# Layer 0's MLP with both token streams in shared tiles and joint groups of 512 columns

## The chip, the cores and the metric

The kernel runs on one core of one Trainium2 chip. The metric is device time in microseconds of one execution; several executions are timed and their median is given. One further execution is profiled, and all rows in this document come from such profiles. TensorE multiplies matrices and writes PSUM, VectorE (DVE) and ScalarE (ACT) do elementwise work, GpSimd (POOL) does little here, and SyncE (SP) issues the DMAs.

## The reference

A backbone of two layers works on two streams of 256 tokens each with 1024 channels: context tokens and latent tokens. Each layer has a mixing part (three head groups: differential attention, latent attention, an RWKV-7 scan) and then a channel part, a gated MLP with a centred convolution of width 3 over the tokens:

```python
def conv_ffn(h, P):
    u = dwconv3(h @ P['ffn_w_up'], P['ffn_conv_w'], P['ffn_conv_b'])
    g, v = jnp.split(u, 2, axis=-1)
    return (jax.nn.silu(g) * v) @ P['ffn_w_down']
```

The up weight has 1024 rows and 2 x 2816 columns, the down weight 2816 rows and 1024 columns. Both streams use the same weights of a layer, each with its own normalisation and modulation before it. Latents read the context in the mixing part, the context never reads the latents, and after layer 1 only the latents are returned, so layer 0 runs its MLP on both streams and layer 1 only on the latents.

## The kernel before, in words

**Layout and arithmetic.** Channels lie on the 128 partitions, tokens on the free axis. Every fp32 operand is split in a high part `h` and a low part `lo` of the type fp32r, and a product is three matmuls, high by high, high by low, low by high (`mm3`, lines 277 to 279). A weight tile of 128x1024 is loaded by SyncE, cast to its high part on ScalarE (line 269) and subtracted to its low part on VectorE (line 270), in `wgroup`.

**The MLP's groups.** `ffn` (line 1176) goes through 22 groups `i` of 128 gate columns and the 128 value columns that belong to them. For each group it makes g (8 k-tiles x 3 matmuls), then v (the same), into one PSUM bank: g in columns 0 to 255, v in 256 to 511. `tap3` (line 449) reads each half out of PSUM: one activation with scale and bias on ScalarE (line 454) and two multiply-adds with shifted tokens on VectorE (lines 457 and 458). Then come silu on ScalarE (1244), the product on VectorE (1245), a cast to the high part (223) and the low part (1247), which give the group's "act". Two groups later the act is multiplied with its 128 rows of the down weight (`push`, `second`): 4 quarters (2 token halves x 2 column halves, one accumulating bank each) x 3 matmuls of 512 columns. The last four rows of the down weight are held to the end and then done quarter by quarter; each quarter ends with `finish`.

**The two streams.** The first call, `ffn(0, hc, ...)`, runs all 22 groups for the context. Beside it a generator (`Side`, line 1266) does what is left of the latents' mixing part, five steps for each group, and ends with the latents' own normalisation (`normed` at line 1541, `norm_mod` at line 405), which makes `hl`. From group `JOIN` = 11 on, that generator is run to its end, and each group is done for both streams with one loading and splitting of the up weights: the context's g and v in a bank of tag `g`, the latents' in a bank of tag `r`. The order within such a group is g of the context, g of the latents, v of the context, v of the latents, each of 24 matmuls with 256 moving columns. Acts of the latents are kept in tiles of tag `al`. The second call, `ffn(0, hl, ..., early=ahead)`, does the latents' groups 0 to 10 and takes the other acts from there; beside it the context's part of layer 1 runs.

**Memory.** `hc` and `hl` of layer 0 are four tiles each, `[128, 4, 256]`, two k-tiles of high and of low part in one (`stream_h`, line 399). Tags name groups of buffers, `BUFS` (line 103) their counts; PSUM has two banks of tag `g`, two of `r`, four of `acc` (the quarters) besides those of the attention (`PB`, line 108).

**What sets the order.** The program's text names no order between engines. A planner takes all instructions with modelled costs, starts on each engine what is ready and most urgent, and places tiles of all tags in one memory by lifetimes; a tile that needs a buffer waits for its release. So independent chains are interleaved on an engine. The resulting order on each engine is fixed in the program. Accesses to parts of one SBUF tile that don't overlap are not ordered against each other; in PSUM, accesses to one bank are. Some loads are tied to a matmul by hand: the loads of layer 1's first weights wait for the last up matmul of the fourth group from the end (`marks[-4]`, group 18).

Of the kernel before, what the change touches and what calls it, by code (L numbers as in the profile page):

```python
# [10 lines left out]
F32 = mybir.dt.float32  # L11
F32R = mybir.dt.float32r
I32 = mybir.dt.int32
AF = mybir.ActivationFunctionType
ALU = mybir.AluOpType
# [4 lines left out]
P = 128  # L20
DM = 1024
KT = DM // P
# [69 lines left out]
def tile_trunk(ctx: ExitStack, tc, A, out):  # L92
# [7 lines left out]
        uid[0] += 1  # L100
        return f"{s}_{uid[0]}"

    BUFS = dict(h=8, hc=4, hl=4, otc=4, otl=4, wrs=13, wrm=3, whm=3, wlm=4, wro=4, who=5, wlo=3, wra=4, wrf=3, whf=4, wlf=6, at=4, al=4, c4=12, d4=12, rk=4, xsc=2, xsd=2, xn=2, nf=5, xs=4, ar=3, gv=3, pa=8, oh=2, sh=3, ob=1, stc=3, std=1, xt=4, gt=2, qk=2, qz=4, va=2, bm=3, lx=1, wx=1, vb=1, bq=3, pc=4)

    def T(tag, shape, dt=F32, pool=None):
        return sb.tile(shape, dt, tag=tag, name=nm(tag), bufs=BUFS[tag])

# [291 lines left out]
    def stream_h(tag):  # L399

        ts = [T(tag, [P, 4, SQ], F32R) for _ in range(KT // 2)]
        hs = [(t[:, 0:2], t[:, 2:4], t.bitcast(F32)[:, 0:2]) for t in ts]
        return hs, [(ts[k // 2][:, k % 2], ts[k // 2][:, 2 + k % 2]) for k in range(KT)]

    def norm_mod(hs, xns, sc, tags):

# [769 lines left out]
    def ffn(l, hk, gate, fill, other=None, early={}, begin=(0, nofill)):  # L1176
# [35 lines left out]
            else:  # L1212
                second(k, wg, quads)

        def place(name, tag):

            n, _, _ = slots.get(name, (0, 0, 0))
            if n % 2 == 0:
                gv, at = T("gv", [P, 4, SQ]), T(tag, [P, 4, SQ], F32R)
            else:  # L1220
                _, gv, at = slots[name]
            slots[name] = n + 1, gv, at
            n %= 2
            return gv[:, n * 2], gv[:, n * 2 + 1], at[:, n], at[:, 2 + n], at.bitcast(F32)[:, n]

        for n, i in enumerate(todo):
            if n == begin[0]:
                begin[1]()
                turn[0] = "acc"
                acc.extend([PS("acc") for _ in range(2)] for _ in range(2))  # L1230
            streams = [(hk, PS("g"), place(0, "at"), acts)]
            h2 = other(i) if other else None
            if h2:
                streams.append((h2, PS("r"), place(1, "al"), ahead))
            for gi, m in enumerate((i, NFF + i)):
                wg = wgroup(A["ffn_w_up"][l][:, m * P : (m + 1) * P].rearrange("(k p) c -> p k c", p=P), KT, P)
                for x, ps, at, _ in streams:
                    for k in range(KT):
                        ins = mm3(ps[:, gi * SQ : (gi + 1) * SQ], (wg[0][:, k, :], wg[1][:, k, :]), x[k], k == 0, k == KT - 1)
                    tap3(ps[:, gi * SQ : (gi + 1) * SQ], at[gi], 1, PPc(l, "cw0", m), PPc(l, "cw1", m), PPc(l, "cw2", m),  # L1240
                         PPc(l, "cb", m))
            marks.append(ins)
            for _, _, (g, v, h, lo, hf), res in streams:
                S.activation(g, g, AF.Silu)
                V.tensor_tensor(g, g, v, ALU.mult)
                copy("ffh", h, g)
                V.tensor_tensor(lo, g, hf, ALU.subtract)
                res[i] = h, lo
            fill()
            for k in order[n]:  # L1250
                push(k)
# [57 lines left out]
                V.scalar_tensor_tensor(xs[j], pcs[j], r[:, i : i + 1], xs[j], ALU.mult, ALU.add)  # L1309
        return xs  # L1310

    def normed(l, s, pcs, ssq, base, gname, tag, tags, each=False):
        xns = normalise(close(s, pcs, ssq, each), "xn", each)
        sc = modulation(l, base, gname, s)
        hs, hk = stream_h(tag)
        norm_mod(hs, xns, sc, tags)
        return hk

# [191 lines left out]
    def after_context(late):  # L1510

        saved = list(phase)
        phase[:] = ["o", late, 0]
        for ti in (0, 1):
            load_x(ti, True, late)
        gt = gate_tile(0, 2, CTX, late)
        out0["wo"], pcs, ssq = run(w_out(0, oTs[CTX], W0, gt, WO))
        for _ in range(NB):
            queue.append((1, (2, 3, 0, 1, 4, 5)[out0.setdefault("ada", 0)]))
            out0["ada"] += 1  # L1520
            fill()
        out0["hc"] = normed(0, CTX, pcs, ssq, 3, "fpre", "hc", NT, EA)
        turn[0] = HB
        phase[:] = saved

# [4 lines left out]
    def latents0():  # L1530
        while not (heads.done and mixing.done):
            heads.step()
            mixing.step(MIX)
            yield
        late = chain[LAT]
        phase[:] = ["o", late, 0]
        for ti in (2, 3):
            load_x(ti, True, late)
        gt = gate_tile(0, 2, LAT, late)
        late, pcs, ssq = yield from w_out(0, oTs[LAT], "r", gt, (2, 0, 1, 3))  # L1540
        return normed(0, LAT, pcs, ssq, 3, "fpre", "hl", ("r",), EB)


    hc, wo = out0["hc"], out0["wo"]
# [3 lines left out]
    def fill_side(n):  # L1548
        def f():
# [5 lines left out]
    agate[:] = [wo, 0]  # L1555
    queue.extend((1, ch) for ch in (2, 3, 0, 1, 4, 5)[NB:])
    marks, pcs, ssq, ahead = ffn(0, hc, lambda ins: gate_tile(0, 5, CTX, ins), fill_side(SB),
                                lambda i: side.run() if i >= JOIN else None, begin=(ACC0, heads.run))
    hl = side.run()


# [126 lines left out]
```

## Time and profile before

| | |
|---|---|
| time before, median of 3 runs | 1360.2 us (1359.5 to 1369.34) |
| the profiled execution's own time | 1361.95 us |
| its span, first to last instruction | 1360.1 us |
| mean granted TensorE clock | 0.981 of full speed |
| TensorE busy | 1285.8 us (95%) |
| VectorE busy | 965.8 us (71%) |
| ScalarE busy | 696.1 us (51%) |
| first joint matmul of the latents | 553.34 us after the start |
| last one of them | 702.38 us |

Busy time of an engine is the time in which it has an instruction running; matmuls overlap, so their durations add up to more than it. "Idle before" in a row is the time for which the engine had nothing, and behind the arrow stands what ended it. The granted clock is that of TensorE, 1.00 for its full speed.

### The profile page before, as it was taken

To read this page: it belongs to the slowest core of one execution; us is meant where nothing else is said; L and a number is where in the kernel's file an instruction comes from. 1 tells how busy PE (TensorE), PEld (TensorE's weight loads), DVE (VectorE), ACT (ScalarE), POOL (GpSimd) and SP (SyncE) were. 2 spreads that over 40 slices of the span, in tenths; PEclk is the share of its full clock that TensorE was granted. 3 is DMA by queue.
4 is the path that set the end of the run, shared out by engine and by line. 5 is a ranking of instruction groups with operands and counts; after the bars stand their busy time and mean duration, and the time that the engine had idled before them with its cause. 6 is when DMAs were issued, how large, how long until landed. Compare 5 with 4: busy or idle time off the path is not lost.

```text
span 1360.1 us, 27958 instructions
## 1 busy us (share of the span) xinstructions
PE 1285.8 (95%) x11208; PEld 1079.1 (79%) x11208; DVE 965.8 (71%) x2438; ACT 696.1 (51%) x1368; POOL 21.1 (2%) x41
## 2 busy tenths in 40 slices
PE   5999999998989999999999999999998997999997
PEld 4787766665777888999999888889865775999996
DVE  3548667657679587866769579587869587777776
ACT  4335244765664554534446555655545654555553
POOL 0001000000000000000000000000100000000000
PEclk9999899997999999999999999999998998999999
DMA  9830265300886565432557446447220048456662
GB/s 323 273 108 16 62 178 183 116 1 2 299 283 189 168 218 170 130 118 78 163 184 224 140 152 206 138 122 214 63 63 1 2 138 265 140 170 202 186 183 81
DMA packets 216531, 202.50 MB, mean 149 GB/s; under 512 B 7825, under 2 KB 175313, under 8 KB 216401
## 3 DMA queue, kind: packets, MB, share of 16 engines
q1 hardware_dynamic: 216400, 200.71, 47.6%
q8 instruction: 88, 1.44, 0.4%
q14 instruction: 43, 0.34, 0.1%
HBM read 198.55 MB, written 2.13 MB: 148 GB/s over the span
## 4 chain that ended last, share of the span: by engine, by line
PE 79%; DVE 13%; ACT 4%; issue 2%; DMA 1%; SPq 0%; POOL 0%; ACTq 0%; DVEq 0%; POOLq 0%
PE g L277 10%; PE g L279 10%; PE g L278 10%; PE acc L277 7%; PE acc L279 7%; PE acc L278 7%; PE r L277 3%; PE r L279 3%; PE r L278 3%; PE acc L906 3%; PE g L1103 2%; PE acc L902 1%; PE r L770 1%; PE r L789 1%; PE acc L322 1%
## 5 line engine op out<-in xcount | busy, mean ns | idle before, releaser
L270 DVE TENSOR_TENSOR wlf<-wrf,whf 128x1024 fp32r<-128x1024 f32 x176 | 214.3, 1220 | 58.8 <-ACT whf L269 37.2
L269 ACT ACTIVATE whf<-wrf 128x1024 fp32r<-128x1024 f32 x176 | 184.6, 1051 | 31.2 <-DMA wrf<-in_ffn_w_up_dram 8.6
L277 PE MATMUL g<-hl,whf 128*128 128x256 f32 x528 | 149.7, 285 | 0.9 <-DVE gv L458 0.8
L278 PE MATMUL g<-hl,whf 128*128 128x256 f32 x528 | 148.9, 284 | 0.0
L279 PE MATMUL g<-hl,wlf 128*128 128x256 f32 x528 | 147.0, 284 | 0.1
L454 ACT ACTIVATE gv<-g,pers 128x256 f32<-128x256 f32 x110 | 61.9, 563 | 155.6 <-PE g L279 154.6
L277 PEld LDWEIGHTS g<-hl,whf 128*128 128x128 f32 x528 | 100.9, 191 | 4.8 <-issue 2.2
L278 PEld LDWEIGHTS g<-hl,whf 128*128 128x128 f32 x528 | 101.0, 191 | 1.9 <-issue 0.3
L277 PE MATMUL g<-hc,whf 128*128 128x256 f32 x352 | 100.6, 286 | 1.6 <-DVE gv L458 0.9
L278 PE MATMUL g<-hc,whf 128*128 128x256 f32 x352 | 100.4, 285 | 0.0
L279 PEld LDWEIGHTS g<-hl,wlf 128*128 128x128 f32 x528 | 99.7, 191 | 1.0 <-issue 0.3
L279 PE MATMUL g<-hc,wlf 128*128 128x256 f32 x352 | 100.0, 285 | 0.0
L457 DVE SCALAR_TENSOR_TENSOR gv<-g,pers,gv 128x255 f32<-128x255 f32 x110 | 52.7, 479 | 65.5 <-ACT gv L454 65.5
L270 DVE TENSOR_TENSOR wlm<-wrm,whm 128x1024 fp32r<-128x1024 f32 (+2 forms) x64 | 71.9, 1132 | 33.3 <-ACT whm L269 19.6
L277 PE MATMUL acc<-whf,at 128*128 128x512 f32 x220 | 87.9, 402 | 0.4 <-ACT ar L344 0.4
L278 PE MATMUL acc<-wlf,at 128*128 128x512 f32 x220 | 87.5, 398 | 0.6 <-DVE wlf L270 0.6
L279 PE MATMUL acc<-whf,at 128*128 128x512 f32 x220 | 86.8, 395 | 0.1
L269 ACT ACTIVATE whm<-wrm 128x1024 fp32r<-128x1024 f32 (+2 forms) x64 | 62.5, 987 | 38.8 <-PE acc L279 17.4
L277 PEld LDWEIGHTS g<-hc,whf 128*128 128x128 f32 x352 | 67.2, 191 | 4.5 <-issue 2.5
L278 PEld LDWEIGHTS g<-hc,whf 128*128 128x128 f32 x352 | 67.2, 191 | 1.5 <-issue 0.2
L279 PEld LDWEIGHTS g<-hc,wlf 128*128 128x128 f32 x352 | 67.1, 191 | 0.4
L895 ACT ACTIVATE pa<-g,pers 128x512 f32<-128x512 f32 (+1 forms) x72 | 44.2, 615 | 32.9 <-DVE pers L894 32.4
(534 smaller groups left out, 3434.4 us busy)
## 6 DMA issues: line engine op xcount, KB each, us to landing
wrf<-in_ffn_w_up_dram SPq DMA_DIRECT2D x110, 512.0 KB
wra<-in_ada_w_dram SPq DMA_DIRECT2D x80, 512.0 KB
wrf<-in_ffn_w_down_dram SPq DMA_DIRECT2D x66, 512.0 KB
wrm<-in_w_in_dram SPq DMA_DIRECT2D x52, 512.0 KB
wro<-in_w_out_dram SPq DMA_DIRECT2D x24, 512.0 KB
wrs<-in_ada_w_dram SPq DMA_DIRECT2D x32, 256.0 KB
gt<-gate SPq DMA_DIRECT2D x6, 512.0 KB
wrm<-in_w_in_dram SPq DMA_DIRECT2D x8, 352.0 KB
```

The lines of the kernel that those rows point to most:

```text
L269: S.activation(h[:, :n], raw[:, :n], AF.Copy)
L270: V.tensor_tensor(lo[:, :n], raw[:, :n], h.bitcast(F32)[:, :n], ALU.subtract)
L277: first = TE.matmul(ps, lh[0], rh[0], start=start, stop=False)
L278: TE.matmul(ps, lh[0], rh[1], start=False, stop=False)
L279: TE.matmul(ps, lh[1], rh[0], start=False, stop=stop)
L322: ins = TE.matmul(ps[q * 32 : q * 32 + 32, :], ca[:, k, :], ws[k // 2][:, c0 : c0 + P], start=k == 0, stop=k == KT - 1)
L454: S.activation(o[:, : n * SQ], ps[:, : n * SQ], AF.Identity, scale=wc, bias=bias)
L457: V.scalar_tensor_tensor(o3[:, :, 1:SQ], p3[:, :, 0 : SQ - 1], wp, o3[:, :, 1:SQ], ALU.mult, ALU.add)
L770: chain[s] = TE.matmul(px[eo * 64 : eo * 64 + 64, pd, :], sc[:, pd, eo, 0:64], SV[:, pd, eo, :], start=True, stop=True)
L895: S.activation(pr_[:, :nk], ps[:, :nk], AF.Exp, bias=m, accum_out=sm)
L906: TE.matmul(po[:, :width], pT[:, b * P : (b + 1) * P], vtiles[b], start=(b == 0), stop=(b == nb - 1))
L1103: ins = TE.matmul(ps[:, :nk], qT[:, i, qc : qc + P], kT_[:, :nk], start=True, stop=True)
```

## The change

Layer 0's normalised input of both streams goes into shared tiles: `both_h` makes four pairs of tiles of a new tag `hj`, `[128, stream, k-tile, 256]`, one of a pair for high, one for low parts. Each stream has its view for its own normalisation and its own groups, and a third view takes a k-tile of both streams as 2 x 256 columns, with a gap between the two runs. `hj` has 8 buffers; `hc` and `hl` are used from layer 1 on.

In groups 11 to 21 a matmul now streams that third view, 512 columns, so that a group has 2 x 24 matmuls. The bank of tag `g` holds g of both streams, the bank of tag `r` holds v of both. Taps, activation and product run once over 512 columns in a new tile `[128, 2, 512]` of tag `gv`; cast and low part are still made per stream, into the same `at` and `al` tiles. The groups of one stream alone are as before.

```diff
--- before.py
+++ after.py
@@ -100,7 +100,7 @@
         uid[0] += 1
         return f"{s}_{uid[0]}"
 
-    BUFS = dict(h=8, hc=4, hl=4, otc=4, ...)
+    BUFS = dict(h=8, hc=4, hl=4, hj=8, otc=4, ...)
 
     def T(tag, shape, dt=F32, pool=None):
         return sb.tile(shape, dt, tag=tag, name=nm(tag), bufs=BUFS[tag])
@@ -401,6 +401,14 @@
         ts = [T(tag, [P, 4, SQ], F32R) for _ in range(KT // 2)]
         hs = [(t[:, 0:2], t[:, 2:4], t.bitcast(F32)[:, 0:2]) for t in ts]
         return hs, [(ts[k // 2][:, k % 2], ts[k // 2][:, 2 + k % 2]) for k in range(KT)]
+
+    def both_h():
+
+
+        ts = [(T("hj", [P, 2, 2, SQ], F32R), T("hj", [P, 2, 2, SQ], F32R)) for _ in range(KT // 2)]
+        views = [([(h[:, s], lo[:, s], h.bitcast(F32)[:, s]) for h, lo in ts],
+                  [(ts[k // 2][0][:, s, k % 2], ts[k // 2][1][:, s, k % 2]) for k in range(KT)]) for s in (CTX, LAT)]
+        return views, [(ts[k // 2][0][:, :, k % 2], ts[k // 2][1][:, :, k % 2]) for k in range(KT)]
 
     def norm_mod(hs, xns, sc, tags):
 
@@ -1212,39 +1220,50 @@
             else:
                 second(k, wg, quads)
 
-        def place(name, tag):
+        def place(name, tag, wide=False):
 
             n, _, _ = slots.get(name, (0, 0, 0))
             if n % 2 == 0:
-                gv, at = T("gv", [P, 4, SQ]), T(tag, [P, 4, SQ], F32R)
+                gv, at = None if wide else T("gv", [P, 4, SQ]), T(tag, [P, 4, SQ], F32R)
             else:
                 _, gv, at = slots[name]
+                if gv is None and not wide:
+                    gv = T("gv", [P, 4, SQ])
             slots[name] = n + 1, gv, at
             n %= 2
-            return gv[:, n * 2], gv[:, n * 2 + 1], at[:, n], at[:, 2 + n], at.bitcast(F32)[:, n]
+            act = at[:, n], at[:, 2 + n], at.bitcast(F32)[:, n]
+            return act if wide else (gv[:, n * 2], gv[:, n * 2 + 1]) + act
 
         for n, i in enumerate(todo):
             if n == begin[0]:
                 begin[1]()
                 turn[0] = "acc"
                 acc.extend([PS("acc") for _ in range(2)] for _ in range(2))
-            streams = [(hk, PS("g"), place(0, "at"), acts)]
-            h2 = other(i) if other else None
-            if h2:
-                streams.append((h2, PS("r"), place(1, "al"), ahead))
-            for gi, m in enumerate((i, NFF + i)):
+            both = other(i) if other else None
+            if both:
+                gv = T("gv", [P, 2, 512])
+                g, v = gv[:, 0], gv[:, 1]
+                outs = [(place(0, "at", True), acts), (place(1, "al", True), ahead)]
+                parts = [(PS("g"), g), (PS("r"), v)]
+            else:
+                g, v, *act = place(0, "at")
+                outs = [(act, acts)]
+                ps = PS("g")
+                parts = [(ps[:, 0:SQ], g), (ps[:, SQ:512], v)]
+            x, seqs = (both, 2) if both else (hk, 1)
+            for m, (ps, to) in zip((i, NFF + i), parts):
                 wg = wgroup(A["ffn_w_up"][l][:, m * P : (m + 1) * P].rearrange("(k p) c -> p k c", p=P), KT, P)
-                for x, ps, at, _ in streams:
-                    for k in range(KT):
-                        ins = mm3(ps[:, gi * SQ : (gi + 1) * SQ], (wg[0][:, k, :], wg[1][:, k, :]), x[k], k == 0, k == KT - 1)
-                    tap3(ps[:, gi * SQ : (gi + 1) * SQ], at[gi], 1, PPc(l, "cw0", m), PPc(l, "cw1", m), PPc(l, "cw2", m),
-                         PPc(l, "cb", m))
+                for k in range(KT):
+                    to_ = ps.rearrange("p (s t) -> p s t", s=2) if both else ps
+                    ins = mm3(to_, (wg[0][:, k, :], wg[1][:, k, :]), x[k], k == 0, k == KT - 1)
+                tap3(ps, to, seqs, PPc(l, "cw0", m), PPc(l, "cw1", m), PPc(l, "cw2", m), PPc(l, "cb", m))
             marks.append(ins)
-            for _, _, (g, v, h, lo, hf), res in streams:
-                S.activation(g, g, AF.Silu)
-                V.tensor_tensor(g, g, v, ALU.mult)
-                copy("ffh", h, g)
-                V.tensor_tensor(lo, g, hf, ALU.subtract)
+            S.activation(g, g, AF.Silu)
+            V.tensor_tensor(g, g, v, ALU.mult)
+            for s, ((h, lo, hf), res) in enumerate(outs):
+                gs = g[:, s * SQ : (s + 1) * SQ]
+                copy("ffh", h, gs)
+                V.tensor_tensor(lo, gs, hf, ALU.subtract)
                 res[i] = h, lo
             fill()
             for k in order[n]:
@@ -1309,10 +1328,10 @@
                 V.scalar_tensor_tensor(xs[j], pcs[j], r[:, i : i + 1], xs[j], ALU.mult, ALU.add)
         return xs
 
-    def normed(l, s, pcs, ssq, base, gname, tag, tags, each=False):
+    def normed(l, s, pcs, ssq, base, gname, tag, tags, each=False, into=None):
         xns = normalise(close(s, pcs, ssq, each), "xn", each)
         sc = modulation(l, base, gname, s)
-        hs, hk = stream_h(tag)
+        hs, hk = into or stream_h(tag)
         norm_mod(hs, xns, sc, tags)
         return hk
 
@@ -1519,7 +1538,8 @@
             queue.append((1, (2, 3, 0, 1, 4, 5)[out0.setdefault("ada", 0)]))
             out0["ada"] += 1
             fill()
-        out0["hc"] = normed(0, CTX, pcs, ssq, 3, "fpre", "hc", NT, EA)
+        out0["views"], out0["joint"] = both_h()
+        out0["hc"] = normed(0, CTX, pcs, ssq, 3, "fpre", "hc", NT, EA, out0["views"][CTX])
         turn[0] = HB
         phase[:] = saved
 
@@ -1538,7 +1558,7 @@
             load_x(ti, True, late)
         gt = gate_tile(0, 2, LAT, late)
         late, pcs, ssq = yield from w_out(0, oTs[LAT], "r", gt, (2, 0, 1, 3))
-        return normed(0, LAT, pcs, ssq, 3, "fpre", "hl", ("r",), EB)
+        return normed(0, LAT, pcs, ssq, 3, "fpre", "hl", ("r",), EB, out0["views"][LAT])
 
 
     hc, wo = out0["hc"], out0["wo"]
@@ -1555,7 +1575,7 @@
     agate[:] = [wo, 0]
     queue.extend((1, ch) for ch in (2, 3, 0, 1, 4, 5)[NB:])
     marks, pcs, ssq, ahead = ffn(0, hc, lambda ins: gate_tile(0, 5, CTX, ins), fill_side(SB),
-                                lambda i: side.run() if i >= JOIN else None, begin=(ACC0, heads.run))
+                                lambda i: (side.run(), out0["joint"])[1] if i >= JOIN else None, begin=(ACC0, heads.run))
     hl = side.run()
```

## Rows read from the trace of the kernel before

**Rows 1.** The page: busy time of each engine, share of the span, instructions.

```profile
PE 1285.8 (95%) x11208; PEld 1079.1 (79%) x11208; DVE 965.8 (71%) x2438; ACT 696.1 (51%) x1368; POOL 21.1 (2%) x41
```

**Rows 2.** Stretches: length, busy PE, PEld, DVE, ACT, POOL (count), granted clock, DMA share, GB/s.

```profile
581.00:595.00 14.00, 14.00 (x108) 13.50 (x108) 9.41 (x17) 5.72 (x9) 0.00 (x0) 1.00 0.42 133
...
860.00:890.00 30.00, 30.00 (x292) 25.25 (x289) 20.50 (x39) 16.67 (x30) 0.00 (x0) 1.00 0.55 163
```

**Rows 3.** Groups of instructions, 553 to 703 us: busy us, mean ns | idle before.

```profile
L277 PE MATMUL r<-hl,whf 128*128 128x256 f32 x176 | 49.7, 282 | 0.0
L277 PE MATMUL g<-hc,whf 128*128 128x256 f32 x168 | 47.6, 283 | 0.9 <-DVE gv L458 0.9
...
L454 ACT ACTIVATE gv<-g,pers 128x256 f32<-128x256 f32 x22 | 12.4, 564 | 50.1 <-PE g L279 50.1
...
L457 DVE SCALAR_TENSOR_TENSOR gv<-g,pers,gv 128x255 f32<-128x255 f32 x22 | 10.6, 483 | 28.3 <-ACT gv L454 28.3
```

**Rows 4.** Timeline of PE, a joint group: start us, duration us, instruction.

```profile
590.03 0.40 PE L279 MATMUL acc<-whf,at 128*128 128x512 f32 x1
...
592.10 0.39 PE L279 MATMUL acc<-whf,at 128*128 128x512 f32 x1
592.33 0.28 PE L277 MATMUL g<-hc,whf 128*128 128x256 f32 x1
...
600.84 0.28 PE L279 MATMUL g<-hc,wlf 128*128 128x256 f32 x1
```

**Rows 5.** Timeline of PE, layer 0's input projection over both streams.

```profile
286.73 0.39 PE L277 MATMUL g<-h,whm 128*128 128x512 f32 x1
...
293.31 0.39 PE L279 MATMUL g<-h,wlm 128*128 128x512 f32 x1
```

**Rows 6.** Timeline of all engines where the latents join.

```profile
547.43 0.28 PE L279 MATMUL g<-hc,wlf 128*128 128x256 f32 x1
...
549.61 1.22 DVE L270 TENSOR_TENSOR wlf<-wrf,whf 128x1024 fp32r<-128x1024 f32 x1
...
549.75 0.87 PE L389 MATMUL r<-pers,xn 128*128 128x128 f32 x6
...
551.41 0.40 PE L277 MATMUL acc<-whf,at 128*128 128x512 f32 x1
...
552.18 0.68 DVE L417 TENSOR_TENSOR hl<-nf,hl 128x512 fp32r<-128x512 f32 x1
...
553.34 0.28 PE L277 MATMUL r<-hl,whf 128*128 128x256 f32 x1
```

**Rows 7.** Timeline of all engines around TensorE's hole in group 19.

```profile
667.42 1.06 ACT L269 ACTIVATE whm<-wrm 128x1024 fp32r<-128x1024 f32 x1 [0.78 <-DMA wrm<-in_w_in_dram]
...
671.12 0.36 PE L277 MATMUL g<-hc,whf 128*128 128x256 f32 x1 [0.92 <-DVE gv L458]
```

**Rows 8.** Groups of instructions, whole span: operations over 512 columns elsewhere.

```profile
L895 ACT ACTIVATE pa<-g,pers 128x512 f32<-128x512 f32 x48 | 32.9, 686 | 25.9 <-DVE pers L894 25.6
...
L1109 DVE SCALAR_TENSOR_TENSOR pa<-pa,pers 128x512 f32<-128x512 f32 x16 | 11.9, 746 | 0.2
```

**Rows 9.** Timeline of all engines at the end of the joint groups.

```profile
701.80 0.43 DVE L1247 TENSOR_TENSOR at<-gv,at 128x256 fp32r<-128x256 f32 x1
...
702.50 0.40 PE L279 MATMUL acc<-whf,at 128*128 128x512 f32 x1
```

**Rows 10.** Stretches in which TensorE had little to do, and what followed.

```profile
322.00:324.00 2.00, 0.40 (x6) 0.16 (x6) 1.81 (x10) 0.77 (x3) 0.00 (x0) 1.00 0.00 0
328.00:332.00 4.00, 3.94 (x34) 2.95 (x30) 2.11 (x4) 2.39 (x6) 0.00 (x0) 0.50 0.02 4
...
388.00:390.00 2.00, 0.49 (x3) 0.31 (x3) 1.86 (x6) 0.00 (x0) 0.00 (x0) 1.00 1.05 387
```

**Rows 11.** Waits: total us, times, longest; TensorE's over the span, ScalarE's in 700:960.

```profile
PE g L1103 <- DVE qz L889: 5.0, 1, 5.0
...
ACT whf L269 <- DMA wrf<-in_ffn_w_down_dram: 3.4, 1, 3.4
```

More of the change, by code (lines that the diff above doesn't have):

```diff
@@ L101, in nm @@
         return f"{s}_{uid[0]}"
-    BUFS = dict(h=8, hc=4, hl=4, otc=4, otl=4, wrs=13, wrm=3, whm=3, wlm=4, wro=4, who=5, wlo=3, wra=4, wrf=3, whf=4, wlf=6, at=4, al=4, c4=12, d4=12, rk=4, xsc=2, xsd=2, xn=2, nf=5, xs=4, ar=3, gv=3, pa=8, oh=2, sh=3, ob=1, stc=3, std=1, xt=4, gt=2, qk=2, qz=4, va=2, bm=3, lx=1, wx=1, vb=1, bq=3, pc=4)
+    BUFS = dict(h=8, hc=4, hl=4, hj=8, otc=4, otl=4, wrs=13, wrm=3, whm=3, wlm=4, wro=4, who=5, wlo=3, wra=4, wrf=3, whf=4, wlf=6, at=4, al=4, c4=12, d4=12, rk=4, xsc=2, xsd=2, xn=2, nf=5, xs=4, ar=3, gv=3, pa=8, oh=2, sh=3, ob=1, stc=3, std=1, xt=4, gt=2, qk=2, qz=4, va=2, bm=3, lx=1, wx=1, vb=1, bq=3, pc=4)
     def T(tag, shape, dt=F32, pool=None):
```

## The prediction

> **What bounds the kernel now.** I first read the busy shares of the page: TensorE has work for 95% of the span, VectorE for 71%, ScalarE for 51% [rows 1]. TensorE is therefore the first suspect, but a share over the span is no proof, so I next cut the stage that the diff touches into stretches [rows 2]. In 581 to 595 us, a stretch of the joint groups, TensorE is busy 14.00 of 14.00 us at a granted clock of 1.00, VectorE 9.41, ScalarE 5.72 and the DMA share is 0.42. In the second MLP, 860 to 890 us, TensorE is busy 30.00 of 30.00. So in this stage time is the sum of what TensorE streams, plus a few holes, and work taken from VectorE or ScalarE is worth nothing by itself.
>
> Third, how much is streamed. By the groups of instructions from 553 to 703 us [rows 3], the latent half is 3 lines x 176 matmuls of 256 columns = 528 = 11 groups x 48, and the context half the same (3 x 168 in the window; the other 24 ran before it). The page's mean of 0.28 us for one is a latency; since matmuls overlap, the price is the step from start to start. Two rows with 71 steps between them, 592.33 and 600.84 us, give 8.51 / 71 = 0.1199 us for 256 columns [rows 4].
>
> **The change, part by part.**
>
> *Wide matmuls.* In each of 11 groups 96 matmuls of 256 columns become 48 of 512. No row shows a joint matmul of this stage. The nearest are the input projection's, which stream 512 columns of a normalised input past a weight into one bank: 29 steps from 286.73 to 293.31 us, 6.58 / 29 = 0.2269 us [rows 5]. The down products, also 512 wide, give a second price: 9 steps from 590.03 to 592.10 us, 0.230 us [rows 4]. I take 0.2269, because stationary weight, moving activation and a long chain into one bank are the same there; the down products swap the operands. Gain: 48 x (2 x 0.1199 - 0.2269) = 48 x 0.0129 = 0.62 us per group, x 11 = **-6.8 us** (with 0.230: -5.2). The new moving operand is two runs of 256 with a gap. If that made it as dear as two matmuls the gain would be 0, which is the other end.
>
> [...]
>
> *The join.* Now a cost that the diff doesn't show. Group 11 is the first joint one. Before, its context half needs only hc, and TensorE streams those 24 matmuls (from 547.43 us to the down product at 551.41) while the latents' norm ends beside it: transposes at 549.75 us, the first low part of hl at 552.18 with 0.68 us, the first matmul on hl at 553.34 [rows 6]. After, a joint matmul needs both halves, so this cover is gone: 24 x 0.1199 = 2.9 us. What else can fill it? The 12 down products that before start at 551.41 us; four of them ran before 553.34, so eight, 8 x 0.23 = 1.8 us, could come forward. But their weight's low part is only made by the split at 549.61 + 1.22 = 550.83 us [rows 6], behind the norm's own work on VectorE. From 547.43 until the transposes of 549.75 TensorE has next to nothing: 2.3 us. Taken: **+2.3 us**; ends 2.9 - 1.8 = +1.1 and +2.9.
>
> *Banks.* Before, g and v of one stream share a bank, so v's matmuls wait for the taps that read g. Normally the other stream's 24 matmuls cover this; once they don't. A cast waits until 667.42 us for its DMA at the head of ScalarE's queue, the tap behind it is late, and TensorE stands 0.92 us, until 671.12, for the tap's last pass on VectorE [rows 7]. After, g and v of a joint group have a bank each, and a bank comes round two groups later. The DMA stays as late, since its loads still wait for the last up matmul of group 18; the tap still queues behind the cast, but nothing on TensorE waits for it. **-0.9 us**; ends -0.9 and 0.
>
> *Taps and activation.* Per joint group ScalarE gives up four taps of 0.56 us for two of 512 columns, 0.69 us each by the 512-column ACTIVATE from PSUM: 2.24 against 1.38 us. VectorE gives up eight tap passes of 0.48 us for four of 0.75: 3.9 against 3.0 us [rows 3, 8]. Activation and product are halved in number too; cast and low-part subtraction stay as they were, per stream. All of it runs beside full matmuls: 0. If TensorE were no longer full, VectorE would have over 4 us to spare in each group [rows 2]. Nothing is put on the SP or POOL queue.
>
> *The tail.* The last context act used to be ready at 701.80 + 0.43 us; the held down products start at 702.50, when the up matmuls are through [rows 9]. After, act 21 is made from a v that ends with the group: tap 0.69 + 2 x 0.75, product at most 0.75, cast and subtraction at most 0.43 each [rows 8, 9], 3.8 us later, and I say 4 with the hand-overs. The held products of rows 18 to 20 need no act 21: 9 per quarter, 36 x 0.23 = 8.3 us over the four quarters. If the planner takes these first the cost is 0. If it keeps quarter by quarter, TensorE waits about 4 - 9 x 0.23 = 1.9 us. I take 0, since the planner does interleave chains [rows 6]; ends 0 and +1.9.
>
> *Shared tiles.* hj is 8 tiles of 4 KB for each partition. Before, hc's four are free when the joint groups end; now the halves are freed together, so 16 KB more are held before the join and again from about 703 us to 894. Nothing in the trace before waits on this; priced as a rival, 0 in the sum.
>
> **Sum:** -6.8 + 2.3 - 0.9 = **-5.4 us**. The profiled execution took 1361.95 us around a span of 1360.1, so that run would become 1356.6. It lies 1.75 us above the median of the runs, 1360.2, from which the same sum gives **1354.8 us**.
>
> **Rivals.**
>
> *The wide matmul is no cheaper*: 512 columns in two runs cost twice 256, or nearly. Against it, the input projection's 0.2269 [rows 5]; for it, that no row has a moving operand with a gap. Sum +2.3 - 0.9 = +1.4: 1361.6 us. Chance 0.08.
>
> *The clock falls at the join.* [...] Chance 0.15. [...]
>
> *Slower: the space held by hj makes weights late in the second MLP.* [...] The one late load there is a cast that waits 3.4 us for its down weight [rows 11], with TensorE covered. Were two of them uncovered, 6.8 us, it would be slower than before; that is the point from which it decides. Four give 1354.8 + 13.6 = 1368.4 us. For it: nothing is released early any more. Against: TensorE has 30.00 of 30.00 us of work there [rows 2], and scan tiles can wait as well. [...] Chance 0.15.
>
> *The planner finds another order.* Costs and lifetimes change, so instructions far away may move. The waits of TensorE that one order has and another needn't have are up to 5.0 us, at the attention's queries [rows 11]. One such wait less makes it 1349.8, one more 1359.8. Chance 0.17, two thirds of it on the good side.
>
> **How the numbers follow.** The forecast itself, 1354.8, has 0.45; its own terms span -6.8 + 1.1 - 0.9 = -6.6 (1353.6) to -5.2 + 2.9 + 1.9 = -0.4 (1359.8). To leave out no more than 2 in 10 the range goes down past the good order, 1349.8, by the 0.7 us that the lowest run lies under the median and a second, smaller wait, to 1347. Upwards it takes the clock and two to three late weights, 1354.8 + 3 x 3.4 = 1365, to 1366. About 1% (13.6 us) is what a measurement of this kernel can tell from no change. Faster by more needs 1346.6, below every case but two good orders at once: 0.06. Slower by more needs 1373.8, the late weights with a fallen clock: 0.06. Within: 0.88.
>
> **What would show it.** In the profile after: joint matmuls on g and r, 528 in all, with steps of about 0.227 us (0.24: the wide price is wrong); the groups repeating every 48 x 0.227 + 12 x 0.23 = 13.65 us against 48 x 0.24 + 2.77 = 14.28; a hole of about 2.3 us before the first joint matmul, with the granted clock still 1.00 behind it; no wait of the matmuls on L458 between the joint groups; no hole in the down products after the last joint group. The forecast is wrong if the second MLP shows waits on casts or loads, or if the difference lies outside the stretch from 545 to 715 us.

## The result: 1.1% slower

The changed kernel takes 1377.4 us (median) against 1362.9 for the kernel before in the same comparison: +14.5 us, ratio 1.0113, 95% interval 1.0088 to 1.0138. The prediction was 1354.8, range 1347 to 1366, so the time is outside the range and on the other side. The profiled execution took 1376.03 us around a span of 1374.0. Three runs of later comparisons (one each of e5 and e6, one of the kernel before) took 1566 to 2036 us at a mean clock of 0.56 to 0.75 and are left out of the differences below; with them e4's would be +8.7, the figure from which e8's expectation starts.

Where the joint groups run, the forecast held. The first two fences show, of the profile after, the line of the page that answers to [rows 1], and rows of TensorE's timeline.

```profile
PE 1282.3 (93%) x10680; PEld 1056.6 (77%) x10680; DVE 957.3 (70%) x2383; ACT 688.5 (50%) x1335; POOL 21.1 (2%) x41
```

TensorE, VectorE and ScalarE each have less work than before, and the span is 13.9 us longer: the time is in waits, and in the clock.

```profile
390.16 0.38 PE L277 MATMUL g<-hj,whf 128*128 128x256 f32 x1
...
436.77 1.98 PE L725 MATMUL r<-d,d 32*32 32x32 f32 x64 [2.66 <-DVE d L708]
...
439.63 0.28 PE L734 MATMUL r<-d,d 32*32 32x32 f32 x2 [0.88 <-ACT whf L269]
...
514.38 0.50 PE L277 MATMUL r<-who,otl 128*128 128x512 f32 x1
...
549.61 0.36 PE L277 MATMUL g<-hj,whf 128*128 128x256 f32 x1 [1.51 <-DVE pers L237]
...
693.24 0.39 PE L277 MATMUL r<-hj,whf 128*128 128x512 f32 x1
...
698.68 0.39 PE L277 MATMUL acc<-whf,at 128*128 128x512 f32 x1
...
710.48 0.38 PE L277 MATMUL g<-hj,whf 128*128 128x256 f32 x1 [0.76 <-ACT whf L269]
...
711.74 0.39 PE L279 MATMUL g<-hj,wlf 128*128 128x256 f32 x1 [0.76 <-DVE wlf L270]
...
722.82 0.50 PE L278 MATMUL acc<-wlf,al 128*128 128x512 f32 x1 [1.03 <-DVE wlf L270]
...
729.16 0.55 PE L277 MATMUL g<-hj,whf 128*128 128x256 f32 x1 [4.21 <-DVE gv L466]
...
916.57 0.33 PE L972 MATMUL r<-pers,pa 128*128 128x128 f32 x1 [0.98 <-DVE pa L230]
```

From 693.24 to 698.68 lie the 24 joint matmuls of one half group: 5.44 / 24 = 0.2267 us each. The holes in square brackets stand elsewhere: before the join, and in the second MLP.

Three starts that both kernels have serve as landmarks: the context's first up matmul (390.16; before 392.32), the latents' output projection (514.38; before 510.51), and the first of layer 1's latent attention (916.57; before 902.59). I call the first interval *early* (before: 118.19 us) and the second *late* (before: 392.08 us). After, they take 124.22 and 402.19 us: early +6.0, late +10.1. The profile after was 2.2 us ahead at the first landmark, which makes up the balance to +14; up to there the clock was at 0.50 for 20.5 us, in the profile before for 27.3.

### The profile page after: what moved, and what is told of

It reads as the page before. It is cut to its first block, busy times and chain, and to the rows that moved or that the text cites. A ratio compares the mean times of both kernels' runs of the same rounds, so it can differ in the third digit from the quotient of the medians.

```text
span 1374.0 us, 26829 instructions
## 1 busy us (share of the span) xinstructions
PE 1282.3 (93%) x10680; PEld 1056.6 (77%) x10680; DVE 957.3 (70%) x2383; ACT 688.5 (50%) x1335; POOL 21.1 (2%) x41
## 4 chain that ended last, share of the span: by engine, by line
PE 73%; DVE 15%; ACT 5%; DMA 4%; issue 2%; SPq 0%; POOL 0%; DVEq 0%; ACTq 0%; POOLq 0%
PE g L277 10%; PE g L279 10%; PE g L278 10%; PE acc L278 6%; PE acc L277 6%; PE acc L279 6%; PE r L278 3%; PE r L277 3%; PE r L279 3%; PE acc L914 2%; DVE wlf L270 2%; PE g L1111 2%; DMA wro<-in_w_out_dram 1%; DVE c L703 1%; PE acc L910 1%
## 5 line engine op out<-in xcount | busy, mean ns | idle before, releaser
L270 DVE TENSOR_TENSOR wlf<-wrf,whf 128x1024 fp32r<-128x1024 f32 x176 | 214.4, 1220 | 66.4 <-ACT whf L269 39.8
L277 PE MATMUL g<-hj,whf 128*128 128x256 f32 (+1 forms) x440 | 138.3, 314 | 9.0 <-DVE gv L466 6.7
L279 PE MATMUL g<-hj,wlf 128*128 128x256 f32 (+1 forms) x440 | 137.0, 312 | 2.3 <-DVE wlf L270 2.2
L462 ACT ACTIVATE gv<-g,pers 128x256 f32<-128x256 f32 (+1 forms) x99 | 58.0, 587 | 160.9 <-PE g L279 159.8
L278 PE MATMUL g<-hj,whf 128*128 128x256 f32 (+1 forms) x440 | 137.2, 312 | 0.0
L277 PEld LDWEIGHTS g<-hj,whf 128*128 128x128 f32 x440 | 86.1, 196 | 17.2 <-issue 7.2
L278 PE MATMUL g<-hl,whf 128*128 128x256 f32 x352 | 98.8, 283 | 0.0
L277 PE MATMUL g<-hl,whf 128*128 128x256 f32 x352 | 98.7, 283 | 0.2 <-DVE gv L466 0.2
L279 PE MATMUL g<-hl,wlf 128*128 128x256 f32 x352 | 96.5, 283 | 0.0
L465 DVE SCALAR_TENSOR_TENSOR gv<-g,pers,gv 128x255 f32<-128x255 f32 (+1 forms) x99 | 50.3, 508 | 65.9 <-ACT gv L462 65.7
L279 PEld LDWEIGHTS g<-hj,wlf 128*128 128x128 f32 x440 | 85.7, 195 | 7.2 <-DVE wlf L270 2.9
L278 PEld LDWEIGHTS g<-hj,whf 128*128 128x128 f32 x440 | 86.0, 195 | 5.6 <-issue 0.5
L277 PEld LDWEIGHTS g<-hl,whf 128*128 128x128 f32 x352 | 67.4, 192 | 1.3 <-issue 0.6
L278 PEld LDWEIGHTS g<-hl,whf 128*128 128x128 f32 x352 | 67.5, 192 | 0.9 <-DVE hl L425 0.2
L279 PEld LDWEIGHTS g<-hl,wlf 128*128 128x128 f32 x352 | 66.1, 192 | 0.0
```

What stands on the lines that cost most here:

```text
L270: V.tensor_tensor(lo[:, :n], raw[:, :n], h.bitcast(F32)[:, :n], ALU.subtract)
L277: first = TE.matmul(ps, lh[0], rh[0], start=start, stop=False)
L278: TE.matmul(ps, lh[0], rh[1], start=False, stop=False)
L279: TE.matmul(ps, lh[1], rh[0], start=False, stop=stop)
L462: S.activation(o[:, : n * SQ], ps[:, : n * SQ], AF.Identity, scale=wc, bias=bias)
L465: V.scalar_tensor_tensor(o3[:, :, 1:SQ], p3[:, :, 0 : SQ - 1], wp, o3[:, :, 1:SQ], ALU.mult, ALU.add)
```

## Experiments

Differences of medians are against the kernel before, run beside each. "Early" and "late" are the two intervals above in each kernel's profile, against the kernel before's; these are single executions, and part of both is the clock (all of "early" in e2 hold late and e8, where the clock is low at 388 to 400 us). So the last two columns have the clock: for how long it was at 0.50 within early and within late in the profile, and, over all runs, span times the missing share of the mean clock (1 less the clock), median, and behind the stroke the same of the kernel before beside it. What a us of it costs is worked out below, at e6.

| kernel | median, us | ratio, 95% interval | early | late | at 0.50, us | missing, us |
|---|---|---|---|---|---|---|
| changed | +14.5 | 1.0113, 1.0088 to 1.0138 | +6.0 | +10.1 | 13.7, 13.7 | 38.5 / not on record |
| e1 tiles only | +10.1 | 1.0088, 1.0055 to 1.0121 | +6.0 | +9.6 | 13.7, 3.4 | 32.2 / 29.3 |
| e2 hold early | +0.4 | 0.9998, 0.9977 to 1.0019 | -2.2 | +0.2 | 1.1, 0 | 32.1 / 29.3 |
| e2 hold late | +6.4 | 1.0050, 1.0032 to 1.0068 | +3.1 | +8.3 | 7.5, 6.8 | 32.2 / 29.3 |
| e3 give back | +6.7 | 1.0056, 1.0034 to 1.0078 | +0.2 | +3.7 | 0.4, 6.8 | 34.2 / 29.3 |
| e4 changed, gv 4 | +9.3 | 1.0069, 1.0043 to 1.0095 | +6.0 | +2.9 | 13.7, 3.4 | 35.6 / 27.2 |
| **e5 give back, gv 4** | **-4.9** | **0.9959, 0.9934 to 0.9983** | 0.0 | -3.8 | 0, 0 | 24.4 / 27.2 |
| e6 hold early, exact | +6.4 | 1.0046, 1.0020 to 1.0071 | +11.4 | +0.2 | 27.3, 0 | 32.8 / 27.2 |
| e7 before, gv 2 | +6.8 | 1.0053, 1.0029 to 1.0076 | 0.0 | +7.7 | 0, 10.2 | 30.1 / 27.2 |
| e8 gv 4, early back | +7.9 | 1.0054, 1.0031 to 1.0078 | +5.0 | +3.9 | 11.6, 3.4 | 32.8 / 27.2 |
| e9 gv 4, late back | +4.2 | 1.0025, 1.0001 to 1.0050 | +12.0 | -3.3 | 27.3, 3.4 | 37.5 / 27.2 |
| e10 give back, al 6 | -0.4 | 0.9998, 0.9974 to 1.0023 | 0.0 | -4.8 | 0, 0 | 27.9 / 27.2 |
| e11 hold late, whole | +6.4 | 1.0045, 1.0023 to 1.0067 | 0.0 | +8.9 | 0, 3.4 | 27.4 / 30.0 |

### Space, or the order? (e1, e2, e3)

Theory M, from the prediction's slower rival: the 16 KB more that hj holds. Rival O: the planner's order, upset by the wide groups.

**e1** has the shared tiles and nothing else of the change:

```diff
-        out0["hc"] = normed(0, CTX, pcs, ssq, 3, "fpre", "hc", NT, EA)
+        out0["views"], out0["joint"] = both_h()
+        out0["hc"] = normed(0, CTX, pcs, ssq, 3, "fpre", "hc", NT, EA, out0["views"][CTX])
 ...
```

> The shared tiles of both streams alone: hj as in the changed kernel, but the joint groups as before, 256 moving columns and taps per stream. Theory M (space): the 16 KB more that hj holds, from the context's norm to the join and again through the second MLP, cost all of the loss, and the wide groups give their gain (offset of matched work +4.5 us at 549 us, -2.5 at 718, so about -7). Then this kernel has the loss without the gain: before + 14.5 + 7 = before + 21 us (15 to 28). Rival O (order): the new costs of wide matmuls and taps make the planner choose another order and the tiles do nothing: before, within 3 us.

Measured +10.1, under M's range of 15 to 28. That refutes O as the only cause: no matmul is wide here. But 21 was too much; something in the second MLP is the changed kernel's alone. The 4.21 us hole before a tap is one thing that e1 does not have.

**e2 hold early** and **e2 hold late** add only unused tiles to the kernel before, e.g.

```diff
+    hold = [T("hd", [P, 1024]) for _ in range(4)]
+    for t in hold:
+        G.tensor_copy(t[:, 0:1], ahead[21][1][:, 0:1])
 ...
+        after(G.tensor_copy(t[:, 1:2], t[:, 0:1]), marks[-1])
```

> The kernel before, with four tiles of 4 KB that nothing uses, written (one column, on POOL) when the context's norm starts and read when the latents' norm is done, so held from about 391 to 551 us, as the latents' half of hj is. Theory M: the early loss comes with them, about +6 us (+3 to +10), with a hole of TensorE near 434 us. Rival O: within 2 us of before.

> The kernel before, with four unused tiles of 4 KB held from the last joint act to the last up matmul of the second MLP, about 703 to 894 us, as the context's half of hj is. Theory M: the late loss comes with them, +8 by 755 us and +8 more by 903: about +16 us (+8 to +22), with waits of TensorE on casts, splits or tap results. Rival O: within 2 us of before.

The late hold cost +6.4: not nothing, as O had it, but under M's range of +8 to +22. Its write ran only at 792.10 us, so that it held the space for the end of the second MLP alone (e11 holds it for the whole). The early one cost nothing: a miss for M, but its first access ran at 355.86 us, so the 16 KB were taken 36 us ahead of the norm, and the order around the norm came out otherwise. e6 repeats it at the right moment.

**e3** keeps the wide groups and shortens what the space is held for:

```diff
+    def carry(dst, src, first):
+        for (dh, dl, _), (sh_, sl, _) in zip(dst, src):
+            after(G.tensor_copy(dh, sh_), first)
+            after(G.tensor_copy(dl, sl), first)
 ...
+        out0["views"], out0["joint"] = both_h()
+        carry(out0["views"][CTX][0], out0["hs"], late)
+        return normed(0, LAT, ..., out0["views"][LAT])
 ...
+    hs, hl = stream_h("hl")
+    carry(hs, out0["views"][LAT][0], None)
```

> The changed kernel with the space given back: the context's norm writes its own hc tiles as before; hj is made only when the latents' output projection has started (about 514 us), the context's half copied into it on POOL, and the latents' half is copied out to hl tiles on POOL, so that the second MLP holds 16 KB, not 32. Wide groups as changed. Theory M: the loss goes and the gain stays: before - 5 to - 7 us. Rival O: the order still comes from the wide groups, so the loss stays: before + 10 to + 15 us.

Measured +6.7, against both theories: early is cured (+0.2), late is not (+3.7). TensorE still waited 4.01 us for a tap at 730.27 us. So there was another cause besides the space.

### The gv buffers (e4, e5, e7, e10)

The timeline of the profile after around that hole, VectorE and ScalarE:

```profile
725.05 0.49 DVE L223 CAST al<-gv 128x256 fp32r<-128x256 f32 x2
...
725.94 1.00 ACT L462 ACTIVATE gv<-g,pers 128x256 f32<-128x256 f32 x2
```

The matmuls of the second MLP's first g ended by 714.7 us, but their tap (an activation into a gv tile) starts at 725.94; before, it started at 716.37. Just ahead of it two latents' acts are cast out of gv tiles into al tiles. Four al buffers hold acts 11 to 18; 19 to 21 wait until the second MLP has used up an al tile, and until then their products stay in gv. Before, those three lay in two gv tiles (a tile held two groups of one stream), and one of the three buffers was left. After, each joint group has a gv tile of its own, so all three are taken. Theory G.

**e4** and **e5** are the changed kernel and e3 with one number altered; **e7** does the reverse to the kernel before; **e10** gives e3 the al buffers instead:

```diff
-    gv=3        +    gv=4      (e4, e5)
-    gv=3        +    gv=2      (e7, the kernel before)
-    al=4        +    al=6      (e10)
```

> The changed kernel with 4 buffers of tag gv in place of 3, nothing else. New theory G: a joint group's gv tile holds g of both streams, and the latents' acts 19 to 21 cannot be cast before an al buffer comes free (725.05 us), so all three gv buffers are still taken when the second MLP begins, its first tap waits until 725.94 us, and TensorE stands 4.21 us at 729.16. With a fourth buffer that hole goes: 4 to 7 us better than the changed kernel (before + 8 to + 11), the losses at 434 us and from 790 us on stay. Rival (space alone, M): the hole comes from the 16 KB and stays, or comes back elsewhere: before + 14, within 2.

> e3_give_back (hj filled only at the join, the latents' half copied out to hl on POOL) with 4 buffers of tag gv. In e3_give_back TensorE still waited 4.01 us for a tap at 730.27 us. Theories G and M together: both losses gone, the wide groups' gain of 5 to 6 us stays: before - 5, between - 8 and - 3. Rival O (order of the wide groups): the second MLP goes on losing, as in e3_give_back: before + 5 to + 8.

> The kernel before with 2 buffers of tag gv in place of 3, nothing else. There the latents' acts 19 to 21 lie in two gv tiles that wait for an al buffer too (casts at 724 to 791 us), so one of three is left for the second MLP. Theory G: with two none is left, and the second MLP's first taps wait as in the changed kernel: a hole of about 4 us near 725 us, +4 to +8 us. Rival M: nothing, within 2 us.

> e3_give_back with 6 buffers of tag al and 3 of gv, to see what holds the gv tiles. Theory G: the gv buffers are taken because the latents' acts wait for one of 4 al buffers; with 6 they are cast at once, gv comes free, and this kernel equals e5_give_back_gv4: before - 5 (-8 to -3). Rival (three gv buffers are too few for the second MLP by themselves): the 4 us hole near 730 us stays, as in e3_give_back, before + 5 to + 8.

Three of the four medians went G's way, and e10's profile. e4 gained 5.2 us over the changed kernel, and its late interval 7.2. e5, with both cures, is faster than the kernel before by 4.9 us. e7 lost 6.8; its first tap of the second MLP came at 733.00, again just behind the cast into al, which in the kernel before stands at 733.67 us and not at 724 (timeline of e7):

```profile
729.78 0.49 DVE L223 CAST al<-gv 128x256 fp32r<-128x256 f32 x2
...
733.00 1.04 ACT L454 ACTIVATE gv<-g,pers 128x256 f32<-128x256 f32 x2
```

The expected single hole of 4 us did not show there; the loss came in pieces (2.34 us for a weight's cast, until 717.85, the largest) and in the clock, at 0.50 for 10.2 us of late. In e10, with three gv buffers, the tap comes in time (713.03), so it was the al buffers that kept gv taken. e10 ended 0.4 us below the kernel before, not 5: its profile agrees with e5's (late -4.8), its median doesn't and lies outside both expected ranges. Of the 4.5 us between the two medians up to 3 are the clock, by the last column (27.9 against 24.4); the rest is within the intervals.

### Where the 16 KB hurt (e6, e8, e9, e11)

**e6** takes the four tiles where the context's norm makes hc:

```diff
             h, lo, hf = hs[kp]
+            if hold is not None:
+                hold.append(T("hd", [P, 1024]))
+                G.tensor_copy(hold[-1][:, 0:1], full[:, 0, 0:1])
 ...
```

> The kernel before with four unused tiles of 4 KB, each written (one column, on POOL) when the context's norm makes the corresponding hc tile, and read when the latents' norm is done: 16 KB from about 391 to 551 us, as the latents' half of hj. In e2_hold_early the tiles had been taken 36 us earlier. Theory M: the scan's transpose at 400.80 us then waits for a matmul, and TensorE runs out near 434 us: +3 to +8 us. Rival (the early loss is only one order among many that the planner may find): within 2 us of before, no hole at 434.

Measured +6.4, and the same three holes as in the changed kernel. Timeline of TensorE, e6:

```profile
436.44 1.98 PE L720 MATMUL r<-d,d 32*32 32x32 f32 x64 [2.65 <-DVE d L703]
...
439.30 0.28 PE L729 MATMUL r<-d,d 32*32 32x32 f32 x2 [0.88 <-ACT whf L269]
...
439.93 1.28 PE L729 MATMUL r<-d,d 32*32 32x32 f32 x40 [0.35 <-ACT d L723]
```

In the changed kernel the chain begins with VectorE:

```profile
401.88 2.12 DVE L690 STREAM_TRANSPOSE d<-d 128x1024 f32<-128x1024 f32 x1 [3.17 <-PE g L279]
```

The scan's transpose neither reads nor writes anything of the up matmul that it waits for. What is left is the place: its tile lies where that matmul's operand was. (This is inferred from the wait; the trace shows no addresses. In e6 the first link is another: VectorE stands 2.77 us, until 401.56, before the split of a weight whose cast is late, and the transpose follows at 403.09 without a wait of its own. So that the holes come with the space is shown, the link by which they come is not.) The substitution behind it ends some 3 us late (the matmuls that wait for it start at 436.77 us, before at 433.74), and TensorE, which has little else there, runs out: 0.34 of 3.00 us busy in the first row below.

Then the clock. Stretches of the changed kernel (columns as in [rows 2]):

```profile
434.00:437.00 3.00, 0.34 (x11) 0.23 (x12) 2.90 (x7) 0.00 (x0) 0.00 (x0) 1.00 0.72 207
...
440.00:444.00 4.00, 3.74 (x82) 3.56 (x83) 2.88 (x6) 3.56 (x9) 0.00 (x0) 0.50 0.22 37
444.00:448.00 4.00, 4.00 (x27) 3.32 (x27) 0.00 (x0) 1.85 (x7) 0.00 (x0) 0.50 0.94 302
```

and of e6:

```profile
440.00:444.00 4.00, 4.00 (x83) 3.82 (x84) 2.56 (x3) 3.56 (x9) 0.00 (x0) 0.50 0.27 50
444.00:448.00 4.00, 4.00 (x27) 3.25 (x25) 0.00 (x0) 1.88 (x6) 0.00 (x0) 0.50 1.12 329
448.00:464.00 16.00, 16.00 (x113) 12.42 (x112) 6.20 (x11) 6.61 (x16) 0.00 (x0) 0.50 0.25 72
```

The holes themselves are 2.66 + 0.88 + 0.35 = 3.9 us. Behind them TensorE has full streams at a granted clock of 0.50, to about 450 us in the changed kernel, to past 464 in e6. That is the other part of early: +6.0 there, +11.4 here, +12.0 in e9. (e6's profiled run misses 39.8 us of the clock where its median run misses 32.8, so that its median is only +6.4.)

What does a clock of 0.50 cost? Twelve steps of e6 between these two rows of TensorE's timeline:

```profile
461.82 0.41 PE L277 MATMUL g<-hc,whf 128*128 128x256 f32 x1
...
464.38 0.41 PE L277 MATMUL g<-hc,whf 128*128 128x256 f32 x1
```

2.56 / 12 = 0.2133 us for 256 columns, against 0.1199 at 1.00 [rows 4]. By these two steps a us at 0.50 does the work of 0.1199 / 0.2133 = 0.56 us and costs 0.44 in such streams, less where TensorE waits anyway; a us in the table's last column, which is two at 0.50, costs up to 0.88. By that estimate the clock is a large part of most losses: of the changed kernel's 14.5 us up to 7 to 10 (38.5 against the 27.2 to 30.0 of the kernel before), of e6's 6.4 up to 4.9. Much of it falls behind the holes, so it is a cost of the same causes, but one that differs from run to run.

**e8** and **e9** are e4 with one half of e3's cure each:

```diff
 e8: hj made and the context's half copied in at the join; no copy out to hl
 e9: hj made at the context's norm; the latents' half copied out to hl
```

> The changed kernel with 4 gv buffers (e4_gv4, before + 8.7 us) and the early half of the space given back: hj is made and the context's half copied in at the join, but hj's 32 KB stay through the second MLP. Theory M: the hole near 434 us and the fallen clock behind it go, the loss from 735 us on stays: about half of the 13.6 us between e4_gv4 and e5_give_back_gv4, so before + 2 us (0 to +5). Rival (only both halves together change the order): near e4_gv4, before + 7 to + 10.

> The changed kernel with 4 gv buffers and the late half of the space given back: hj is made at the context's norm as in the change, but the latents' half is copied out to hl tiles, so the second MLP holds 16 KB. Theory M: the second MLP runs without the waits on splits, the hole of 2.7 us near 434 us and the fallen clock behind it stay: before + 2 us (-1 to +4). Rival: near e4_gv4, before + 7 to + 10.

e9 came at the edge of what was expected (+4.2). e8 did not: +7.9, 3 us over the range. Its profile has no hole near 434 us, so the cure worked, but there the clock was at 0.50 from 388 to 400 us with TensorE busy 12.00 of 12.00; early is +5.0 by that alone. A loss of that size is usual in e8: its seven runs miss 28.7 to 37.0 us of the clock, 5.6 more at the median than the kernel before beside it. Where in the other runs it falls, and why there, stays open.

**e11** holds the tiles through the whole second MLP of the kernel before:

```diff
+    for t in hold:
+        G.tensor_copy(t[:, 0:1], hl[7][1][:, 0:1])
 ...
```

> The kernel before with four unused tiles of 4 KB written (one column, on POOL) from hl when the latents' norm is done, about 555 us, and read after the last up matmul of the second MLP, about 894 us: through the whole second MLP it holds 16 KB more, as the change does. In e2_hold_late the write had only come at 792 us. Theory M: the late loss is a matter of space, at least the +6.4 us of e2_hold_late and about the 12 us by which e8_early_gv4 is dearer than e5_give_back_gv4: before + 10 us (+6 to +14), waits of TensorE on splits between 735 and 900 us, SP's four wra loads at about 700 us ahead of the down weight's. Rival (those 12 us come from the wide groups' order with the space): before + 2 us or less.

Measured +6.4, at the low end of M's range; in the profile late is +8.9, of which the clock is up to 1.5. TensorE's waits from 703 to 905 us, e11 (total, times, longest):

```profile
PE g L279 <- DVE wlf L270: 2.6, 3, 1.5
PE acc L278 <- DVE wlf L270: 1.9, 1, 1.9
PE g L277 <- DVE gv L458: 1.8, 2, 1.4
PE r L726 <- ACT c L705: 1.0, 1, 1.0
```

The same view of e5, which holds no more there than the kernel before:

```profile
PE r L978 <- DVE pa L230: 1.0, 1, 1.0
...
PE g L277 <- DVE gv L472: 0.5, 1, 0.5
...
PE acc L278 <- DVE wlf L270: 0.3, 1, 0.3
PE g L279 <- DVE wlf L270: 0.2, 1, 0.2
```

Splits of weights (wlf) that were covered are late. SyncE's queue shows one way in which a split comes late. Its timeline in the changed kernel:

```profile
698.42 9.66 SPq L256 DMA_DIRECT2D wra<-in_ada_w_dram  x4
708.39 0.34 SPq L256 DMA_DIRECT2D wrf<-in_ffn_w_down_dram  x1
709.75 2.33 SPq L256 DMA_DIRECT2D wrf<-in_ffn_w_up_dram  x2
```

in e11:

```profile
702.93 8.57 SPq L256 DMA_DIRECT2D wra<-in_ada_w_dram  x4
...
711.81 0.34 SPq L256 DMA_DIRECT2D wrf<-in_ffn_w_down_dram  x1
```

and in e5:

```profile
692.87 0.88 SPq L256 DMA_DIRECT2D wra<-in_ada_w_dram  x2
693.81 0.46 SPq L256 DMA_DIRECT2D wrf<-in_ffn_w_down_dram  x1
694.37 1.08 SPq L256 DMA_DIRECT2D wra<-in_ada_w_dram  x2
```

Four loads of the modulation's weights stand in a row for 8.6 to 9.7 us, and the MLP's next down weight queues behind them. In e1, e4 and e8, which also hold the space from 703 us on, it is the same (9.0, 9.7 and 9.7 us); in e3, e5 and e9, which don't, the four are issued in two pairs of about 1 us.

But little of the loss arises there. Match the 528 up matmuls of the second MLP with those of the kernel before, counted from the second landmark: at the 217th, about 800 us, e11 is 0.5 us behind, e4 6.6 and e5 3.8 ahead; at the last one e11 is 8.9 and e4 2.9 behind, and e5 still 3.8 ahead. e2 hold late, which takes the space only at 792.10 us and issues the four loads in pairs, is 0.6 ahead and then 8.3 behind. So the space costs its 8 to 10 us behind 800 us, where the scan of the context's second layer starts (e4 comes there 2.8 us further ahead than e5, which leaves about 7 in all). Rows of SyncE's and TensorE's timelines there, e11:

```profile
812.75 12.00 SPq L256 DMA_DIRECT2D wrf<-in_ffn_w_up_dram  x2
818.40 0.50 PE L278 MATMUL acc<-wlf,at 128*128 128x512 f32 x1 [1.88 <-DVE wlf L270]
829.62 0.39 PE L279 MATMUL g<-hl,wlf 128*128 128x256 f32 x1 [1.46 <-DVE wlf L270]
```

and e2 hold late:

```profile
812.12 9.42 SPq L256 DMA_DIRECT2D wrf<-in_ffn_w_up_dram  x2
815.08 0.50 PE L278 MATMUL acc<-wlf,at 128*128 128x512 f32 x1 [2.06 <-DVE wlf L270]
826.12 0.39 PE L279 MATMUL g<-hl,wlf 128*128 128x256 f32 x1 [1.47 <-DVE wlf L270]
```

Two loads of up weights take 11.4 to 12.0 us there in the changed kernel, e1, e4, e8 and e11, 9.4 in e2 hold late; the longest pair between 780 and 840 us takes 5.8 in the kernel before. TensorE has the same two holes for splits in all six, of 1.55 to 3.17 and of 1.46 or 1.47 us, and the kernel before has neither. So SyncE's queue stands here too, and here it goes with the loss; that the loads wait for a place in memory is argued, not shown.

**The sum.** Late, by kernels that differ in one thing: space given back, gv enough: -3.8 and -3.3 (e5, e9). Space held, gv enough: +2.9 and +3.9 (e4, e8), so the space costs about 7. Space held, three gv: +10.1, so gv costs 7.2; without the space, e3 less e5, 7.5. So the two costs add: -3.6 + 7 + 7.3 = +10.7 against 10.1 measured. Part of each is the clock: at 0.44 us for each us at 0.50, up to 1.5 us of the space's 7 and 3 to 4.5 of the 7.3 of gv. (In the changed kernel the clock is at 0.50 from 727.3 to 734.2 us, around the end of the 4.21 us hole, and twice more before 909.) Early adds 4 us of holes and 2 to 8 of clock. The medians are less additive: early costs 9.1 us from e5 to e9, but 1.4 from e8 to e4. The clock can account for that: e9's runs miss 13.1 us more of it than e5's, e4's 2.8 more than e8's.

## Why the prediction was wrong

- *Wide matmuls*, -6.8: right. Measured 0.2267 us for a step against 0.2269 taken, so 48 x (2 x 0.1199 - 0.2267) x 11 = -6.9. The step with a gap in the moving operand is no longer than the input projection's without one.
- *The join*, +2.3: too dear. TensorE waited 1.51 us (549.61), where before it had waited 0.29 at 545.69: +1.2, near the lower end. The planner put the up matmuls of v of group 10 and all of the due down products into the gap. The clock stayed at 1.00 there, from 545 to 565 us. The rival of the falling clock had the right loss in the wrong place: the clock fell at the holes before 436.77 and 729.16 us, which the prediction did not have, for 13.7 and 6.8 us. The range upwards also takes in a fall of the clock at the join, which no run shows; what the runs showed is a loss of 4.4 us for ten at 0.50 in full streams, by the steps of e6.
- *Banks*, -0.9, and *the tail*, 0: right. No wait on taps between the joint groups; 48 held down products run without a hole from 698.68 us.
- The joint stage as a whole: from the latents' output projection to the held products 184.30 us, before 191.99 [rows 9 has its end]; two products more are held, 0.46 us. So -7.2 against -5.4.
- *Shared tiles*, "0 in the sum": **the step that failed.** "Nothing in the trace before waits on this" was true and proved nothing, since before the space was used by others. The slower rival named the mechanism and the second MLP, and put it at 13.6 us and 0.15. That four weights would be late was my estimate, and no run shows how full the memory is; by itself the space costs about 7 us there, nearly all of it behind 800 us. But the text also had "16 KB more are held before the join", and priced that nowhere. Its price was 4 us of holes and 2 to 8 us of a fallen clock.
- *Taps and activation*, 0: the second failure. Only engine time was counted. The change also makes one gv tile hold both streams of one group in place of one stream of two, and the context's half is done with long before the latents' half can be cast. That cost 7.3 us: the 4.21 us hole is one part, the clock, with up to 3 to 4.5 us, the other.
- The range ended at 1366, two to three late weights; the chance of slower by over 1% was 0.06. The two costs that were missed come on top of the rival's, and together they decide.
- What I had set down as signs against the forecast, waits on casts or loads in the second MLP and a difference outside 545 to 715 us, are what the profile shows.

e5 is what the change wanted to be: faster than before by 4.9 us, where the forecast had 5.4, for 16 copies on POOL (0.6 to 1.6 us each, at 507 to 514 and 548 to 556 us) and one more gv buffer. That the two numbers are so close is partly luck: e5's runs miss 2.8 us less of the clock than those of the kernel before, which is up to 2.5 of its 4.9 us, and in its profile the two intervals together are 3.8 us shorter.

## What to carry to other kernels

When two tiles become one, the new tile lives from the first one's first write to the last one's last read: list, for each stretch in which only one of the two lived before, who used the space, and price their wait as you would any other. The same holds for a buffer that starts to serve two streams: count how many of its tag are still held by the slower stream when the next stage begins. If the wide access needs the common tile only for a while, copy into it and out of it on an engine with little to do (in e5 POOL, 0.6 to 1.6 us a copy). And price a hole of a busy TensorE with the clock that may fall behind it (here 0.50 for 13.7 us behind the holes at 434 us of the changed kernel, for 27.3 in e6).

## What the runs showed of the hardware

A hole of 2.65 or 2.66 us of TensorE at about 434 us was followed by a granted clock of 0.50 in all five profiles that have it (changed, e1, e4, e6, e9), from 437 to 439 us on; in the other nine the clock stays at 1.00 from 434 to 470 us. Time times the missing share of the clock comes to 6.8 us in three of the five and 13.6 to 13.7 in e6 and e9, with the same instructions behind the hole. How much is lost differs between executions of one kernel too: over the whole span e9's twelve runs miss 24.4 to 43.9 us. At 0.50 a step of 256 columns took 0.2133 us against 0.1199, which is 1.78 times as long and not twice. In the second MLP holes of 4.21 (changed), 4.01 (e3), 2.06 (e2 hold late), 1.90 (e4), 1.88 (e11) and 1.87 us (e1) also had 0.50 around their end or right behind it, for 3.4 to 6.8 us; e8's hole of 3.17 us, until 816.15, did not: the clock stays at 1.00 there from 808 to 850 us. The joint groups' hole of 1.51 us, until 549.61, had no fall behind it (1.00 to 565 us), nor had 388 to 390 us before (1.00 to 410); 322 to 324 us before had one, to 0.50 [rows 10]. So some gaps had a fall behind them and some had none; what decides it was not shown.
